# A hybrid recurrent and convolution layer on Trainium2: GpSimd's share of the first two thirds goes to VectorE and ScalarE, and the last head pair, its solve, the last conv block and the two recurrences are put in another order

## The chip, the cores and the metric

The kernel runs on one core of one Trainium2 chip. The metric is the device time of one execution in microseconds (us). Three runs of the kernel before took 1326.93, 1331.70 and 1330.41 us; the median is 1330.41. A separate execution was profiled, and every duration below comes from that one. The engines are named as the profile names them: PE is TensorE (matmuls) and PEld its weight loads, DVE is VectorE, ACT is ScalarE, POOL is GpSimd, SP is the engine that issues most DMAs. The granted clock is the fraction of TensorE's full clock that the chip allowed in a stretch of time.

## What is computed

One decoder layer over 1024 tokens of width 1024, all in float32: a norm, one input projection, then an eight-head recurrence on one part of the columns and a causal convolution of width 31 on the other, one output projection with a residual, and an MLP.

```python
def rwkv7_recurrence(r, decay, k, v, a_vec, b_vec):
    ...
    def step(S, inp):
        r_t, w_t, k_t, v_t, a_t, b_t = inp
        sa = jnp.einsum('bhvk,bhk->bhv', S, a_t)
        S = S * w_t[:, :, None, :] + sa[..., :, None] * b_t[:, :, None, :] + v_t[..., :, None] * k_t[:, :, None, :]
        y = jnp.einsum('bhvk,bhk->bhv', S, r_t)
        return S, y
...
def reference(x, ...):
    for l in range(DEPTH):
        h = rmsnorm(x, norm_mix_g[l])
        p = h @ w_in[l]
        p_rwkv = p[..., :D_RWKV_IN]
        p_rwkv = p_rwkv + (token_shift(p_rwkv) - p_rwkv) * shift_mu[l]
        p_conv = p[..., D_RWKV_IN:]
        y_rwkv = rwkv7_group(p_rwkv, ...)      # 8 heads of 64, with a group norm and a gate
        y_conv = conformer_conv_group(p_conv, ...)  # gated, 31 taps, layer norm, silu
        x = x + jnp.concatenate([y_rwkv, y_conv], axis=-1) @ w_out[l]
        h = rmsnorm(x, norm_mlp_g[l])
        x = x + jnp.square(jax.nn.relu(h @ w_ff1[l])) @ w_ff2[l]
    return rmsnorm(x, norm_final_g)
```

## The kernel before

**Projections.** A float32 product is made from three products of rounded halves: each operand is split into a high part (a rounded copy, made on ScalarE) and a low part (operand minus high part). `mm3` issues high x high, high x low and low x high for each of eight k-blocks, in matmuls of 128x128 weights by 256 columns. `load_w` (L214) loads 1024x128 input weights (`wraw`), makes `wh` on ScalarE (L219) and `wl` on GpSimd (L220); there are 22 such loads. `load_wout` (L682) does the same for the output weights in 16 pieces of 128x512 (`woh`, and `wol` on GpSimd, L692).

**Convolution.** Each of four conv blocks (`conv_block`, 128 channels) projects two weight blocks, gates them into `h`, and puts 31 taps into a list. `do_taps(n)` emits the next n of them: each is one VectorE instruction over 128x1024 (L317 the first, L319 the others) that adds onto `acc`. A tap that is emitted behind a solve is ordered behind the end of that solve (`gate`). When all taps are done, `conv_norm` (L639) normalises one half of the tokens: PE transposes, statistics on VectorE, scaling on ScalarE, PE transposes back, the activation (L663 to L665), and a split into high and low (`cvh` L668 on ScalarE, `cvl` L669 on GpSimd).

**Heads.** The eight heads are taken as four pairs, each in two halves of the tokens. `mix_block` projects and shifts r, k or v for a pair; `decays` (L390) makes the decay factors `E1` and `Ei`; `stage1` (L418) builds for each chunk of 64 tokens the small matrices that the recurrence needs: `AR` (L425, L426), `KB` (L437 and L439 on VectorE, and through `kq` on GpSimd, L436 and L440), their products `AM` (PE, masked on VectorE L448), the transposed, decayed `KB` called `kt` (a matmul of `KB` with a diagonal matrix `dg`, which GpSimd builds in L456), and a bonus term (L471 to L475, of which L472 on GpSimd). They go to DRAM (`lk_d`, `am_d`, `v_d`, `bon_d`).

**Solves.** The recurrence is computed in chunks, which takes the inverse of a triangular matrix for each. `solve(g)` does it for the two pairs of group g: a first product with `nup` (L501, shown as `Q<-Q,nup`), 60 small VectorE operations (L505 and L507), and a last product (L509). `merge(g, h)` puts the inverses' blocks together for one half of the tokens, through DRAM, with a VectorE transpose (`QT`, L524), 64 tiny matmuls and ScalarE copies.

**The two recurrences.** `step(g)` does one of 16 chunks of group g, each in three dependent hops in `chain` (L570): PE with `L1` then a ScalarE copy (L590), PE with `Th` then a copy (L596), PE with `KB` then a VectorE addition into the next chunk's `rhs` (L601). In the profile the matmuls of group 0 write `ca` and `ya`, those of group 1 `cb` and `yb`; their operands are called `rhs,LK`, `SR,TA` and `rhs,TA`. The state times the decay, `SR` (L585), is GpSimd's. `fetch` loads the chunk's matrices two chunks ahead into rings that both recurrences share (`LK` three buffers, `rhs` and `TA` two each). Recurrence 1 needs `solve(1)` and `merge(1)`, recurrence 0 `solve(0)` and `merge(0)`.

**Output projection and MLP.** `out_first` adds the convolution half onto x, `post` (L606) normalises and gates the recurrence's output (GpSimd adds the bonus, L629), and `out_second` adds that half. The MLP behind it is a blocked product whose operand sums run partly on GpSimd (L1187, L1310).

**What sets the order.** The function calls these pieces in a hand-written sequence near its end (L960 on). A scheduler then reorders instructions between engines by a simulated timeline and by priorities (`solve`, `merge` and `step` have a raised one), and the result is a fixed in-order queue for each engine. PSUM banks are handed out in turn from named cycles (L74).

## Time and profile before

| quantity | value |
|---|---|
| median of three runs | 1330.41 us |
| the profiled execution | 1334.43 us |
| its span, first to last instruction | 1332.7 us |
| PE busy | 1229.8 us (92%) |
| DVE busy | 960.9 us (72%) |
| ACT busy | 539.6 us (40%) |
| POOL busy | 291.1 us (22%) |
| mean granted clock | 0.961 |

The page divides the span into 40 slices of about 33 us. Each digit is the busy share in tenths; `PEclk` is the granted clock in tenths.

```profile
PE   6999899988998859999999999999948899999996
DVE  6379965698999672444669766665428898897997
ACT  6313233322323363333468454545533333433345
POOL 2124143332333153311000000000004324231420
PEclk9999899998998778999999999999978899999999
```

The recurrences and the output projection lie in slices 11 to 20, the MLP behind them. POOL is at work in the first 19 slices and again from slice 31 on.

### The profile page before, as it was taken

How to read it: one execution, taken by the hardware profiler on the slowest of the kernel's cores; microseconds unless marked ns; L12 is line 12 of the kernel's file. 1: busy time of each engine (PE TensorE's matmuls, PEld its weight loads, DVE VectorE, ACT ScalarE, POOL GpSimd, SP SyncE). 2: the span in 40 equal slices, each digit the busy share in tenths (PEclk: the TensorE clock that was granted, in tenths of full speed). 3: DMA queues.
4: the chain of work that ended last, by engine and by line, in shares of the span. 5: the costliest groups of instructions: out<-in, count | busy, mean ns of one | idle time of the engine just before them, and what ended most of it. 6: DMA issues, size and time to landing. Idle time of an engine off the chain costs nothing.

```text
span 1332.7 us, 20860 instructions
## 1 busy us (share of the span) xinstructions
PE 1229.8 (92%) x8171; PEld 1059.0 (79%) x8171; DVE 960.9 (72%) x1440; ACT 539.6 (40%) x937; POOL 291.1 (22%) x181
## 2 busy tenths in 40 slices
PE   6999899988998859999999999999948899999996
PEld 5999788887896748899988788888837688888885
DVE  6379965698999672444669766665428898897997
ACT  6313233322323363333468454545533333433345
POOL 2124143332333153311000000000004324231420
PEclk9999899998998778999999999999978899999999
DMA  5211445525626667536135554543157425223003
GB/s 185 56 48 37 109 112 145 132 72 122 155 59 158 160 162 186 176 112 178 44 110 183 159 162 142 163 134 124 66 167 267 142 80 158 63 81 93 16 1 126
DMA packets 194475, 161.44 MB, mean 121 GB/s; under 512 B 54387, under 2 KB 153785, under 8 KB 194377
## 3 DMA queue, kind: packets, MB, share of 16 engines
q1 hardware_dynamic: 181192, 157.90, 40.0%
q10 hardware_dynamic: 13056, 2.13, 0.9%
q8 instruction: 64, 1.05, 0.3%
q14 instruction: 35, 0.28, 0.1%
q0 software_dynamic: 128, 0.08, 0.0%
HBM read 110.23 MB, written 49.84 MB: 120 GB/s over the span
## 4 chain that ended last, share of the span: by engine, by line
PE 60%; DVE 24%; DMA 7%; issue 4%; ACT 2%; SPq 1%; POOL 1%; DVEq 0%; ACTq 0%
PE ps L96 27%; DVE acc L319 9%; PE yb L96 9%; PE ya L96 8%; PE cb L96 7%; PE ca L96 5%; PE pr L96 3%; DMA lk_d<-kt 2%; DVE Q L507 2%; DVE Qt L505 1%; DVE bl L827 1%; DVE sA L1187 1%; DVE al L827 1%; DVE ta L437 1%; PE ps L99 1%
## 5 line engine op out<-in xcount | busy, mean ns | idle before, releaser
L319 DVE SCALAR_TENSOR_TENSOR acc<-h,cw,acc 128x1024 f32<-128x1024 f32 x120 | 176.8, 1493 | 1.1
L826 ACT ACTIVATE ah<-sA 128x1024 fp32r<-128x1024 f32 x32 | 34.0, 1061 | 135.3 <-PE pr L96 50.1
L96 PE MATMUL ps<-bh,ah 128*128 128x512 f32 x168 | 65.7, 404 | 22.4 <-ACT bh L826 16.5
L220 POOL TENSOR_TENSOR wl<-wraw,wh 128x1024 fp32r<-128x1024 f32 x22 | 56.6, 2572 | 136.1 <-ACT wh L219 136.1
L1187 POOL TENSOR_TENSOR sB<-B,B11e 128x1024 f32<-128x1024 f32 x4 | 11.6, 2890 | 337.5 <-DMA B<-in_w_ff_dram 335.2
L96 PE MATMUL cb<-hh,wh 128*128 128x256 f32 x264 | 79.4, 301 | 5.1 <-DVE k L257 3.1
L96 PE MATMUL cb<-hl,wh 128*128 128x256 f32 x264 | 79.9, 302 | 0.1
L96 PE MATMUL cb<-hh,wl 128*128 128x256 f32 x264 | 77.8, 295 | 0.0
L96 PE MATMUL ps<-bl,ah 128*128 128x512 f32 x168 | 68.1, 405 | 4.0 <-DVE bl L827 3.9
L96 PE MATMUL yb<-hh,wl 128*128 128x256 f32 x248 | 71.5, 288 | 0.0
L96 PE MATMUL yb<-hh,wh 128*128 128x256 f32 x248 | 71.4, 288 | 0.0
L96 PE MATMUL yb<-hl,wh 128*128 128x256 f32 x248 | 71.0, 286 | 0.0
L96 PE MATMUL ps<-bh,al 128*128 128x512 f32 x168 | 67.5, 402 | 0.0
L827 DVE TENSOR_TENSOR al<-sA,ah 128x1024 fp32r<-128x1024 f32 x32 | 50.5, 1580 | 23.6 <-ACT ah L826 23.6
L827 DVE TENSOR_TENSOR w1l<-s,w1h 128x512 fp32r<-128x512 f32 x64 | 43.9, 687 | 24.8 <-ACT w1h L826 24.8
L826 ACT ACTIVATE w1h<-s 128x512 fp32r<-128x512 f32 x64 | 40.3, 632 | 50.5 <-PE ps L96 29.0
L96 PEld LDWEIGHTS cb<-hh,wh 128*128 128x128 f32 x264 | 53.2, 202 | 9.0 <-DVE k L257 3.3
L96 PEld LDWEIGHTS cb<-hl,wh 128*128 128x128 f32 x264 | 53.1, 201 | 4.8 <-issue 4.0
L96 PEld LDWEIGHTS ps<-bh,ah 128*128 128x128 f32 x168 | 32.9, 197 | 30.2 <-ACT bh L826 16.9
L585 POOL TENSOR_TENSOR SR<-rhs,PC 64x256 f32<-64x256 f32 x30 | 28.6, 953 | 124.8 <-DVE rhs L601 104.8
L96 PEld LDWEIGHTS cb<-hh,wl 128*128 128x128 f32 x264 | 53.3, 202 | 2.3 <-issue 2.0
L846 ACT ACTIVATE c<-c 128x512 f32<-128x512 f32 x60 | 38.0, 633 | 38.2 <-DVE c L932 21.5
(460 smaller groups left out, 4008.8 us busy)
## 6 DMA issues: line engine op xcount, KB each, us to landing
w1r<-in_w_ff_dram SPq DMA_DIRECT2D x44, 512.0 KB
hid_d<-c SPq DMA_DIRECT2D x64, 256.0 KB
LK<-lk_d SPq DMA_DIRECT2D x32, 384.0 KB
...
```

Of the source, the lines that this page charges most:

```text
L96: return self._order(PE.matmul(o, lhsT=lhsT, rhs=rhs, start=start, stop=stop, skip_group_check=more))
L99: self._order(PE.transpose(o, in_, identity))
L220: G.tensor_tensor(wl, raw, wh.bitcast(F32), op=ALU.subtract)
L319: return V.scalar_tensor_tensor(accs[cb], h2[:, j:j + T], cw[:, j, cb:cb + 1], accs[cb], op0=ALU.mult, op1=ALU.add)
L437: V.scalar_tensor_tensor(ta, ta, 1.0, Ei, op0=ALU.add, op1=ALU.mult)
L505: V.tensor_tensor(o, Q[:, 0:s, s:s + 1].to_broadcast([R, s, n]), Q[:, s:s + 1, s + 1:32].to_broadcast([R, s, n]), op=ALU.mult)
L507: V.tensor_tensor(Q[:, 0:s, s + 1:32], Q[:, 0:s, s + 1:32], o, op=ALU.add)
L585: G.tensor_tensor(SP, rhs[0:64], PC[:, c, 4 * g:4 * g + 4, None].to_broadcast([C, 4, C]), op=ALU.mult)
L826: S.activation(hi, src, AF.Copy)
L827: V.tensor_tensor(lo, src, hi.bitcast(F32), op=ALU.subtract)
L846: S.activation(c, c if src is None else src, AF.Relu)
L1187: engine.tensor_tensor(t, x, y, op=op)
```

## The change

There are three edits.

1. Every GpSimd arithmetic operation ahead of the MLP becomes a VectorE operation of the same shape: `wl` (22), `kq`, `KB` and `r` (8 each), `SR` (30), `yo` (8), `cvl` (8) and `wol` (16). GpSimd keeps its memsets, masks and DMA issues there, and its sums in the MLP.
2. `dg` goes. Four ScalarE operations per group of four chunks scale `KB` into `kd`, and PE transposes `kd`, where it multiplied `KB` by `dg`.
3. The hand-written order changes. The third conv block's projections move ahead of `solve(0)`. The fourth head pair's projections and stages move ahead of the fourth conv block. `solve(1)` and `merge(1)` come directly behind that block's projections, 23 of its taps behind `merge(1, 0)`'s call, and both convolution norms behind all of these. Recurrence 1 starts before the second convolution norm, its steps alternating with recurrence 0's. The cycles of PSUM banks are narrowed while both run.

```diff
-        G.tensor_tensor(wl, raw, wh.bitcast(F32), op=ALU.subtract)
+        V.tensor_tensor(wl, raw, wh.bitcast(F32), op=ALU.subtract)
...
-            dg = mp.tile([P, 4, P], F32, name="dg", bufs=1)
-            G.tensor_tensor(dg, ident[:, None, :].to_broadcast([P, 4, P]),
-                            E1[:, 4 * q:4 * q + 4, C:C + 1].to_broadcast([P, 4, P]), op=ALU.mult)
+            kd = mp.tile([P, 4, P], F32, name="kd", bufs=1)
+            for c in range(4):
+                S.activation(kd[:, c, :], KB[:, 4 * q + c].rearrange("p j t -> p (j t)"), AF.Copy, scale=E1[:, 4 * q + c, C:C + 1])
             bk = bank("s1")
             for c in range(4):
-                bk.mm(bk.t[:, c * P:(c + 1) * P], KB[:, 4 * q + c].rearrange("p j t -> p (j t)"), dg[:, c, :], True, True)
+                bk.tr(bk.t[:, c * P:(c + 1) * P], kd[:, c, :], ident)
...
-            G.tensor_tensor(SP, rhs[0:64], PC[:, c, 4 * g:4 * g + 4, None].to_broadcast([C, 4, C]), op=ALU.mult)
+            V.tensor_tensor(SP, rhs[0:64], PC[:, c, 4 * g:4 * g + 4, None].to_broadcast([C, 4, C]), op=ALU.mult)
...
     do_taps(2)
+    conv_block(2)
     solve(0, (0, 1))
     merge(0, 0)
     in_banks.append("inb")
-    do_taps(4)
-    do_taps(4)
-    conv_block(2)
+    do_taps(8)
     decays(2, 0)
...
-    conv_block(3)
...
     step(0)
     mix_block(7, (0, 1))
     mix_block(3, (0, 1))
+    step(0)
     mix_block(11, (0, 1))
+    do_taps(15)
+    step(0)
     stage1(3, 0)
     decays(3, 1)
+    step(0)
+    stage1(3, 1)
+    step(0)
+    conv_block(3)
     do_taps(8)
-    stage1(3, 1)
-    step(0)
-    step(0)
+    step(0)
+    solve(1, (0, 1))
+    step(0)
+    merge(1, 0)
+    step(0)
+    do_taps(23)
+    assert not taps
+    step(0)
+    merge(1, 1)
     step(0)
     done_in()
+    cycles["any"] = ("ps", "ps", "ps", "pr")
     ct = open_pool("ct", side="right")
     sc = open_pool("sc", side="right")
     cTs[0] = conv_norm(sc, ct, 0)
     close_pool("sc")
-    solve(1, (0, 1))
+    step(0)
     wo = open_pool("wo", side="right")
     load_wout(wo, wo, (4, 5, 6, 7))
-    merge(1, 0)
-    step(0)
-    merge(1, 1)
-    step(0)
-    step(0)
-    step(0)
+    step(0)
+    step(1)
+    step(0)
+    step(1)
     step(0)
     sc = open_pool("sc", side="right")
     cTs[1] = conv_norm(sc, ct, 1)
...
+    cycles["any"] = ("ps", "ca", "ps", "ya", "ps", "pr")
     out_first(wo, 0, 0)
-    step(1)
-    step(1)
     step(1)
```

**The end of the input projection.** The first two excerpts are TensorE's queue around the end of the input projection. `hh` and `hl` are the halves of the normed input, `wh` and `wl` those of the weights, so `cb<-hh_167,wh` is an input-projection matmul; `ps<-AR,KB` makes `AM`, `ps<-dg,KB` and `ps<-ident,kd` make `kt`, and `ca` and `ya` are recurrence 0. Before:

```order
L96 MATMUL cb<-hh_171,wl 128x256
L96 MATMUL ps<-sqk,sel_684 2x512
L96 MATMUL ca<-rhs,LK 64x64 x4
L96 MATMUL ya<-rhs,LK 64x64 x4
L96 MATMUL ps<-AR,KB 128x128 x11
L96 MATMUL ca<-SR,TA 64x64 x4
L96 MATMUL ps<-AR,KB 128x128 x5
L96 MATMUL ca<-rhs,LK 64x64 x4
L96 MATMUL ya<-rhs,TA 64x64 x4
L96 MATMUL ps<-dg,KB 128x128 x4
```

After, around the last `AR,KB` of the last pair's last half:

```order
L96 MATMUL cb<-hh_167,wh 128x256
L96 MATMUL cb<-hl_168,wh 128x256
L96 MATMUL cb<-hh_167,wl 128x256
L96 MATMUL ps<-AR,KB 128x128 x4
L96 MATMUL cb<-hh_171,wh 128x256
L96 MATMUL cb<-hl_172,wh 128x256
L96 MATMUL ca<-SR,TA 64x64 x4
L96 MATMUL cb<-hh_171,wl 128x256
L96 MATMUL cb<-hh_143,wh 128x256
L99 MATMUL ps<-ident,kd 128x128 x4
```

Before, the last input-projection matmul (the first row) stood ahead of both last stages of the fourth pair, and these had only recurrence steps between their matmuls. Now the fourth conv block's projection stands between them.

**Behind the second solve.** The next two excerpts are VectorE's queue from the last small operation of `solve(1)` on. Before:

```order
L507 TENSOR_TENSOR Q<-Q,Qt 128x30
L509 TENSOR_TENSOR Q<-Q,nup 128x1024
L665 SCALAR_TENSOR_TENSOR hn<-th_5107,hn 128x512
L665 SCALAR_TENSOR_TENSOR hn<-th_5121,hn 128x512
L524 STREAM_TRANSPOSE QT<-QS 128x256
L665 SCALAR_TENSOR_TENSOR hn<-th_5135,hn 128x512
L665 SCALAR_TENSOR_TENSOR hn<-th_5149,hn 128x512
L699 TENSOR_TENSOR x_0_4448<-xr,ps 128x512
L524 STREAM_TRANSPOSE QT<-QS 128x256
L699 TENSOR_TENSOR x_2_4450<-xr,ps 128x512
L601 TENSOR_TENSOR rhs<-cb,SR 64x256 x3
```

After:

```order
L507 TENSOR_TENSOR Q<-Q,Qt 128x30
L509 TENSOR_TENSOR Q<-Q,nup 128x1024
L319 SCALAR_TENSOR_TENSOR acc<-h_4120,cw,acc 128x1024
L601 TENSOR_TENSOR rhs<-ca,SR 64x256
L319 SCALAR_TENSOR_TENSOR acc<-h_4120,cw,acc 128x1024 x4
L524 STREAM_TRANSPOSE QT<-QS 128x256
L319 SCALAR_TENSOR_TENSOR acc<-h_4120,cw,acc 128x1024 x8
L524 STREAM_TRANSPOSE QT<-QS 128x256
L319 SCALAR_TENSOR_TENSOR acc<-h_4120,cw,acc 128x1024
L601 TENSOR_TENSOR rhs<-cb,SR 64x256
L319 SCALAR_TENSOR_TENSOR acc<-h_4120,cw,acc 128x1024
L585 TENSOR_TENSOR SR<-rhs,PC 64x256 x2
```

Before, the end of the second convolution norm (`hn`) and the first additions of the output projection (L699) stood directly behind the solve, since all taps were done. Now 23 taps stand there, with recurrence 1's first addition (`rhs<-cb`) among them; the convolution norms follow behind the taps. In the whole queue, 10 of recurrence 0's additions stood ahead of this solve's first product before, and 4 do now.

**The start of the output projection.** The last two excerpts are TensorE's queue there. `woh` and `wol` are the output weights' halves, `cvh` and `cvl` those of the normed convolution, so `ps<-woh_4690,cvh_4533` is an output-projection matmul; `QT,MX` and `QS,PT` belong to `merge(1, ...)`, and `cb` and `yb` are recurrence 1. Before:

```order
L99 MATMUL ps<-ident,yc_5043 128x128
L96 MATMUL cb<-QT,MX 32x32 x32
L96 MATMUL ps<-woh_4690,cvh_4533 128x256
L96 MATMUL cb<-QS,PT 32x32 x32
L96 MATMUL ps<-wol_4691,cvh_4533 128x256
L96 MATMUL ps<-woh_4690,cvl_4534 128x256
L96 MATMUL ps<-woh_4696,cvh_4547 128x256
L96 MATMUL cb<-rhs,LK 64x64 x4
```

After:

```order
L96 MATMUL cb<-SR,TA 64x64 x4
L99 MATMUL ps<-ident,yc_5165 128x128
L99 MATMUL ps<-ident,yc_5166 128x128
L99 MATMUL ps<-ident,yc_5167 128x128
L99 MATMUL ps<-ident,yc_5168 128x128
L96 MATMUL cb<-rhs,LK 64x64 x4
L96 MATMUL yb<-rhs,TA 64x64 x4
L96 MATMUL ps<-woh_4966,cvh_4855 128x256
```

Before, the first output-projection matmul stood ahead of recurrence 1's first hop. Now eight of that recurrence's additions stand ahead of it, among the transposes of the convolution norms (`ident,yc`).

More of the change, by code (lines that the diff above doesn't have):

```diff
@@ L435, in stage1 @@
         S.activation(kq, ta, AF.Identity, scale=kah[:, p:p + 1], bias=kac[:, p:p + 1])
-        G.tensor_tensor(kq, kq, k, op=ALU.mult)
+        V.tensor_tensor(kq, kq, k, op=ALU.mult)
         V.scalar_tensor_tensor(ta, ta, 1.0, Ei, op0=ALU.add, op1=ALU.mult)
@@ L439, in stage1 @@
         V.scalar_tensor_tensor(KB[:, :, 0, :], c8(k), kr, c8(ta), op0=ALU.mult, op1=ALU.mult)
-        G.tensor_tensor(KB[:, :, 1, :], c8(kq), c8(Ei), op=ALU.mult)
+        V.tensor_tensor(KB[:, :, 1, :], c8(kq), c8(Ei), op=ALU.mult)
         for i in range(2):
@@ L471, in stage1 @@
         S.activation(r, r, AF.Copy, scale=prm("r_k", p))
-        G.tensor_tensor(r, r, kq, op=ALU.mult)
+        V.tensor_tensor(r, r, kq, op=ALU.mult)
         bb = bank("s1")
@@ L628, in post @@
             S.activation(yo[:, p, :], b.t[:, p * P:(p + 1) * P], AF.Identity, scale=prm("ln_x_g", p), bias=prm("ln_x_b", p))
-        G.tensor_tensor(yo, yo, bon, op=ALU.add)
+        V.tensor_tensor(yo, yo, bon, op=ALU.add)
         V.tensor_tensor(yo, yo, bg.t.rearrange("p (n t) -> p n t", n=NP), op=ALU.mult)
@@ L668, in conv_norm @@
             S.activation(ch, hn, AF.Copy)
-            G.tensor_tensor(cl, hn, ch.bitcast(F32), op=ALU.subtract)
+            V.tensor_tensor(cl, hn, ch.bitcast(F32), op=ALU.subtract)
             res.append((ch, cl))
@@ L691, in load_wout @@
                 S.activation(wh, raw, AF.Copy)
-                G.tensor_tensor(wl, raw, wh.bitcast(F32), op=ALU.subtract)
+                V.tensor_tensor(wl, raw, wh.bitcast(F32), op=ALU.subtract)
                 wos[k, n] = wh, wl
@@ L1002, in hymba_layer @@
     stage1(2, 1)
-    do_taps(4)
-    do_taps(4)
-    do_taps(4)
-    do_taps(4)
+    do_taps(16)
     decays(3, 0)
-    do_taps(4)
-    do_taps(4)
-    step(0)
-    do_taps(4)
-    do_taps(3)
-    step(0)
-    step(0)
-    step(0)
-    step(0)
-    conv_block(3)
-    do_taps(4)
-    do_taps(4)
-    do_taps(4)
-    do_taps(4)
-    do_taps(4)
-    do_taps(4)
-    do_taps(3)
     step(0)
@@ L1027, in hymba_layer @@
     mix_block(3, (0, 1))
+    step(0)
     mix_block(11, (0, 1))
+    do_taps(15)
+    step(0)
     stage1(3, 0)
     decays(3, 1)
-    do_taps(8)
+    step(0)
     stage1(3, 1)
     step(0)
+    conv_block(3)
+    do_taps(8)
     step(0)
+    solve(1, (0, 1))
[6 more added lines that the diff above has]
+    merge(1, 1)
     step(0)
     done_in()
+    cycles["any"] = ("ps", "ps", "ps", "pr")
     ct = open_pool("ct", side="right")
@@ L1040, in hymba_layer @@
     close_pool("sc")
-    solve(1, (0, 1))
+    step(0)
     wo = open_pool("wo", side="right")
     load_wout(wo, wo, (4, 5, 6, 7))
-    merge(1, 0)
     step(0)
-    merge(1, 1)
+    step(1)
     step(0)
-    step(0)
-    step(0)
+    step(1)
     step(0)
@@ L1062, in hymba_layer @@
     step(0)
+    assert steps[0] == 16
+    cycles["any"] = ("ps", "ca", "ps", "ya", "ps", "pr")
     out_first(wo, 0, 0)
-    step(1)
-    step(1)
     step(1)
@@ L1077, in hymba_layer @@
     post(op, 1)
-    do_taps(4)
-    do_taps(4)
     out_first(wo, 3, 1)
@@ L1095, in hymba_layer @@
     out_first(wo, 4, 1)
-    do_taps(4)
     step(1)
@@ L1130, in hymba_layer @@
     close_pool("nx")
+    assert steps[1] == 16
     ph2.close()
+    cycles["any"] = ("ps", "ca", "ya", "ps", "cb", "pr", "ps", "yb")
     fpb = open_pool("fpb", side="right")
```

## The prediction

> **What bounds the kernel now.** I read the page's head and its chain of work first, then the busy time of each engine by stage, then who TensorE waited for.
>
> ```profile
> span 1332.7 us, 20860 instructions
> PE 60%; DVE 24%; DMA 7%; issue 4%; ACT 2%; SPq 1%; POOL 1%; DVEq 0%; ACTq 0%
> 0.00:451.45 451.45, 410.59 (x3349) 368.48 (x3350) 351.44 (x457) 141.61 (x273) 136.66 (x97) 0.95 0.41 107
> 451.45:505.03 53.58, 35.72 (x447) 28.37 (x446) 41.50 (x117) 35.07 (x65) 22.97 (x21) 0.80 0.62 165
> 505.03:690.00 184.97, 181.22 (x1756) 168.03 (x1756) 87.33 (x243) 70.43 (x169) 33.18 (x33) 0.99 0.49 139
> 690.00:1332.70 642.70, 602.29 (x2625) 494.10 (x2623) 480.62 (x624) 292.53 (x432) 98.33 (x32) 0.97 0.38 122
> 403.00:451.45 48.45, 41.56 (x326) 32.65 (x325) 37.46 (x40) 13.99 (x30) 13.79 (x13) 0.79 0.60 149
> ```
>
> A row gives the stretch, its length, the busy time of PE, PEld, DVE, ACT and POOL, the granted clock and the DMA share. I cut where the work changes: 403 is the end of the last input-projection matmul, 451.45 the start of the second solve, 505.03 the point from which output-projection matmuls run without gaps, 690 about where the MLP begins. The chain that ended last runs 60% over TensorE and 24% over VectorE, so these two are cut up by stage. TensorE is the bound almost everywhere: 410.6 of 451.5 us, then 181.2 of 185.0. It is not in the second row, 35.7 of 53.6 us at a clock of 0.80, nor in the last row, the end of the first stage: 41.6 of 48.5 at 0.79. The time to be won before the MLP is the time in which TensorE idles or runs at a reduced clock. The MLP keeps its order and its engines, so I cost it at nothing.
>
> ```profile
> PE pr L99 <- DVE xt L233: 10.6, 3, 9.7
> PE ps L96 <- DVE KB L439: 7.0, 4, 2.6
> PE ps L96 <- ACT kt L462: 5.1, 3, 3.6
> PE cb L96 <- DVE QT L524: 4.8, 1, 4.8
> PE ps L96 <- DVE AM L448: 3.6, 2, 2.1
> ```
>
> This is TensorE's waiting up to 660 us (total, times, longest). No row names POOL: GpSimd was never what TensorE waited for last in these rows. What GpSimd costs is seen on VectorE.
>
> ```profile
> L319 DVE SCALAR_TENSOR_TENSOR acc<-h,cw,acc 128x1024 f32<-128x1024 f32 x120 | 176.8, 1493 | 1.1
> L319 DVE SCALAR_TENSOR_TENSOR acc<-h,cw,acc x120: 1239/1276/3533, 75.2 to 435.3; 128x1024 f32<-128x1024 f32 x120
> L437 DVE SCALAR_TENSOR_TENSOR ta<-ta,Ei 128x512 f32<-128x512 f32 x8 | 14.5, 1810 | 0.0
> L437 DVE SCALAR_TENSOR_TENSOR ta<-ta,Ei x8: 675/1222/5904, 113.1 to 429.9; 128x512 f32<-128x512 f32 x8
> ```
>
> The same tap takes 1.24 to 3.5 us, the same L437 0.68 to 5.9 us. Over the typical tap the 120 taps lose 120 x (1493 - 1276) = 26 us; over its shortest, L437 loses 8 x (1810 - 675) = 9 us. So 35 us of VectorE's 480 before 690 is stretching by something beside it, and two-input operations running while GpSimd runs fit that. The Trainium skill, "SBUF — State Buffer", section "Who interferes with whom", says that a VectorE operation with two SBUF inputs and a GpSimd operation that reads SBUF block each other for whole instructions; by that rule up to POOL's 136.7 us before 451 would come back to VectorE, an estimate; the two rows above show 35 of it, and the sum goes by those.
>
> **Edit 1: GpSimd's work goes to VectorE.**
>
> ```profile
> L220 POOL TENSOR_TENSOR wl<-wraw,wh x22: 2354/2438/3456, 10.4 to 379.2; 128x1024 fp32r<-128x1024 f32 x22
> L436 POOL TENSOR_TENSOR kq<-kq,k 128x512 f32<-128x512 f32 x8 | 14.2, 1779 | 35.2 <-ACT kq L435 22.6 <-DVE k L257 12.6
> L585 POOL TENSOR_TENSOR SR<-rhs,PC x30: 606/607/2787, 201.9 to 642.9; 64x256 f32<-64x256 f32 x30
> L692 POOL TENSOR_TENSOR wol<-woraw,woh 128x512 fp32r<-128x512 f32 x16 | 20.7, 1298 | 29.1 <-ACT woh L691 16.8 <-DMA woraw<-in_w_out_dram 4.6 <-DMA xr<-in_x_dram 4.2
> L827 DVE TENSOR_TENSOR al<-A,ah x16: 1208/1217/1226, 1001.4 to 1295.5; 128x1024 fp32r<-128x1024 f32 x16
> L827 DVE TENSOR_TENSOR w1l<-w1r,w1h x48: 673/686/695, 619.9 to 973.5; 128x512 fp32r<-128x512 f32 x48
> L601 DVE TENSOR_TENSOR rhs<-ca,SR x7: 407/417/417, 440.1 to 480.9; 64x256 f32<-64x256 f32 x7
> L601 DVE TENSOR_TENSOR rhs<-cb,SR x10: 406/417/418, 514.3 to 599.7; 64x256 f32<-64x256 f32 x10
> ```
>
> The lower four rows are VectorE doing the same shapes. So VectorE takes on 22 x 1.22 = 26.8 us (wl), 24 x 0.69 = 16.5 us (kq, KB and r), 30 x 0.42 = 12.5 us (SR) and 32 x 0.69 = 22 us (yo, cvl, wol): 78 us, less the 35 us of stretching, net +43 over 690 us (480 to 523, 76%). In the first stage it is 26.8 + 16.5 + some 2 for SR, less nearly all of the 35: about +10 on 351 of 451 us. The cover is TensorE's own 411 us; it holds while no wl sits long behind taps. KB becomes ready earlier, since its two products on the way (kq, KB) take 0.69 instead of some 1.8 us. At the start a wl stands inside the first normalisation's chain (wl starts at 10.4 today, the first scaling at 8.8):
>
> ```profile
> L233 DVE TENSOR_SCALAR xt<-xt,rs x8: 740/746/2222, 8.8 to 30.7; 128x1024 f32<-128x1024 f32 x8
> ```
>
> Waiting for that wl ends at 10.4 + 1.2 = 11.6, some 3 us behind 8.8; the second tile's scaling is late today too, so between 0 and +3.4 us; I take **+1**.
>
> **Edit 2: kd for dg.** The matmuls stay as many and as large (128x128).
>
> ```profile
> L456 POOL TENSOR_TENSOR dg<-ident,E 128x512 f32<-128x512 f32 x16 | 20.5, 1282 | 88.5 <-PE ps L96 50.5 <-ACT E L411 38.0
> L628 ACT ACTIVATE yo<-ca,par x32: 448/458/466, 537.9 to 674.2; 128x128 f32<-128x128 f32 x32
> ```
>
> ScalarE takes 64 more, at most 0.46 us each by L628 (which reads PSUM): 29 us on 142 busy of 451. They stand between KB and the transposes, which dg did not; each stage has two groups of four, 1.8 us a group, hidden where input projection fills TensorE. Only in the fourth pair's last half is little of it left: between 0 and 2 x 1.8 = 3.6 us; I take **0**.
>
> **Edit 3: the order.** In front, the fourth head pair now comes ahead of the last conv block, so that block's matmuls stand between its stages. Today nothing but stages and recurrence steps stand behind 403, and the last row of the first fence prices the hole: 6.9 us idle and 0.21 x 48.5 = 10 us of clock, overlapping in part: 7 to 17 us, I take 14. In the rest of the front, KB's and AM's waits (7.0 + 3.6) and 12 us of reduced clock (0.05 x 451 = 22.6, less those 10) are to be had in part: 0 to 22, I take 9. Together **-23** (7 to 39).
>
> Behind the front, these rows mark today's serial stage:
>
> ```profile
> 451.45 1.53 DVE L501 TENSOR_TENSOR Q<-Q,nup 128x1024 f32<-128x1024 f32 x1 [0.24 <-DMA Q<-am_d]
> 489.97 1.23 DVE L509 TENSOR_TENSOR Q<-Q,nup 128x1024 f32<-128x1024 f32 x1
> 505.03 0.41 PE L96 MATMUL ps<-woh,cvh 128*128 128x256 f32 x1
> 514.28 0.42 DVE L601 TENSOR_TENSOR rhs<-cb,SR 64x256 f32<-64x256 f32 x1
> L507 DVE TENSOR_TENSOR Q<-Q,Qt 128x30 f32<-128x30 f32 (+14 forms) x30 | 12.1, 404 | 0.3
> L505 DVE TENSOR_TENSOR Qt<-Q 128x30 f32<-128x30 f32 (+14 forms) x30 | 11.0, 366 | 0.4
> 455.69 0.68 PE L96 MATMUL ca<-rhs,LK 128*64 128x64 f32 x8 [0.67 <-ACT rhs L596]
> 456.30 0.67 PE L96 MATMUL ya<-rhs,TA 64*64 64x64 f32 x8
> 458.08 0.67 PE L96 MATMUL ca<-SR,TA 64*64 64x64 f32 x8 [0.17 <-ACT SR L590]
> 459.26 0.68 PE L96 MATMUL ca<-rhs,LK 128*64 128x64 f32 x8 [0.51 <-ACT rhs L596]
> ```
>
> Today: solve from 451.5 to 491.2, convolution norm beside it, output projection dense at +53.6; all taps are done at 436. Changed, 32 taps are left when the second solve starts, 9 inside it and 23 held behind it, and the convolution norm comes behind the last tap. On VectorE: the solve's 60 small operations 23.1 us (the L507 and L505 rows), two Q products 2.5, 9 taps at 1.28 = 11.5, eight steps' rhs and SR 16 x 0.42 = 6.7: **44**. Then 23 taps, 29.4, with two QT, four rhs and five SR, 4.7, and a wait of some 2 for the first rhs of the second recurrence (514.3 - 491.2 = 23 us behind the solve today): **36**. Then convolution norm, for which I take the ACT time of today's stage, 35.1, which holds the same two norms and some recurrence copies: **34**. Sum 114, or **+60** on 53.6.
>
> What that buys: the matmuls of one step fill about 2.9 us of the 3.6 from 455.69 to 459.26. Before the second solve only 4 additions of the first recurrence are done instead of 10: 6 x 2.9 = **-17** in a stage where TensorE was the bound. Behind the start of output projection 8 steps of the second recurrence are already done: 8 x 2.9 = **-23** in a stage that was 98% busy; and of its 3.8 us idle I take **-3**. The output weights' loads stand on SP's queue behind fetches that wait for ring buffers; they have the serial stage's length as cover.
>
> Sum: +60 - 17 - 23 - 23 - 3 + 1 = **-5 us**: 1334.4 of the profiled execution (span 1332.7) becomes about 1329. The shown median, 1330.4, lies 4 below that execution, so I write **1325**.
>
> **Rivals.** *Slower: the steps set the serial stage.* VectorE's queue is in order, and eight rhs stand in the solve, eight more before the first output matmul. Today's L601 rows give 6.8 us a step without filler (40.8 us for 6 intervals) and 9.5 beside output projection (85.4 for 9). Decisive are 44/8 = 5.5 us in the solve and (70 - 23)/7 = 6.7 behind it. At 6.8 and 8.2 the stage is 54 + 23 + 57 = 134 instead of 114: +20, **1345** (at 9.5 it is 54 + 23 + 66, or +29: **1354**). For it speaks the clock:
>
> ```profile
> 460.00:480.00 20.00, 15.35 (x168) 12.04 (x167) 19.38 (x46) 15.21 (x28) 10.26 (x9) 1.00 0.40 108
> 480.00:500.00 20.00, 9.13 (x113) 6.93 (x113) 12.68 (x41) 12.19 (x21) 8.73 (x7) 0.60 0.80 213
> 431.32 1.11 PE L96 MATMUL ca<-SR,TA 64*64 64x64 f32 x8
> ```
>
> Where TensorE was half idle the clock was 0.60, and a hop took 1.11 instead of 0.67, so a step's three hops gain 1.3 us. Against it, steps at 15.4 of 20 busy kept 1.00, and ACT and VectorE's norm work is no longer beside the solve. The Trainium skill, "TensorE: Matmul & The Clock Gate", section "HAM oscillation — how this bites in real kernels", says that a gap of about 3.4 us puts the clock at half until work is sustained; taken for all 16 steps of the stage that is 16 x 1.3 = 21 us, or 1346, an estimate, and the row from 460 to 480 shows that steps alone need not fall under it.
>
> *Faster: VectorE's relief reaches TensorE.* If the front gives 39 instead of 23, and the serial stage's taps run at their 1.24 minimum (32 x 0.04 = 1) with no wait for the first rhs (2), the result is 19 lower: **1306**. For it: the stretched L437 stands directly ahead of KB, TensorE's largest wait after the start. Against: TensorE is at 95% clock and 91% busy there already.
>
> *Nothing or a little slower: VectorE's queue takes what GpSimd gave.* A wl behind one tap comes up to 1.28 us later, 22 times, 28 us at most; it decides once wl is later than TensorE's weight order needs. If the front then gives 8 instead of 23, the result is 15 higher: **1340**.
>
> **How the numbers follow.** About 0.5%, 6.7 us, is what a measurement can tell from no change. Forecast 0.44 (1314 to 1336), of which 0.26 is faster by more than that and 0.18 within it; the faster rival 0.18; steps 0.22, of which 0.02 within 0.5%; VectorE's queue 0.16, of which 0.06. So faster 0.44, same 0.26 (0.18 + 0.02 + 0.06), slower 0.30. The range takes in the slow rival at 9.5 us a step with 3 us of kd's bound (1357), and the faster one with a norm part a third shorter, since ScalarE's 35 us hold copies and weights that are not the norm's, and with the start at 0 instead of +1 (1306 - 11 - 1 = 1294, set at 1290): 1290 to 1357.
>
> **What would show it.** Hardly a POOL row ahead of the MLP; the tap's mean near 1.28; L437 near 0.7; the clock near 1.00 from the end of the front's waits to the second solve, and that start near 412 (451.5 - 17 - 23 + 1). Then 32 taps behind it, the first dense output matmul some 114 us later (526), and 159 us instead of 185 from there to the MLP. The step rival shows as VectorE idle for `ca` or `cb` inside the solve, with rhs rows over 6 us apart; the queue rival as TensorE waiting for wl. Wrong altogether would be a start of the solve behind 430, or an MLP of other length than 643 us.

## The result, and the profile after

The changed kernel takes 1312.62 us in the median of four runs (1312.27 to 1315.79), the kernel before 1331.03 beside it. The ratio is 0.9873, with a 95% interval from 0.9848 to 0.9899: 1.3% faster. The forecast was 1325, 0.4% faster, with 1290 to 1357 as its range. The profiled execution's span is 1310.6 us, 22.1 less than before. One run of those below is left out as slow, 1420.88 us at a granted clock of 0.82 in `e5_no_kd`, whose median is that of the other nine.

First the head of the page after, its chain of work and two rows of the slices (POOL and the clock, then a digit for each fortieth of the span).

```profile
span 1310.6 us, 20752 instructions
PE 82%; DVE 6%; DMA 6%; ACT 3%; issue 1%; SPq 1%; ACTq 0%; DVEq 0%
POOL 1000000000000000000000000000004324232320
PEclk9999999999996588999999999999978899999998
```

VectorE's share of the chain that ended last fell from 24% to 6%, and TensorE's rose from 60% to 82%: ahead of the second solve, TensorE waits for only some 7 us in all behind its first wait. The clock row has lost its dips in slices 5 and 10. Slices 13 to 16, 8 7 7 8 before, are 6 5 8 8 now: the new serial stage lies there.

Next the busy time by stage after: the stretch, its length, PE, PEld, DVE, ACT and POOL busy, the granted clock and the DMA share. I cut at the second solve's start (385.5) and end (427.5), the end of the last tap (461.7), the output projection and about where the MLP begins.

```profile
0.00:385.50 385.50, 364.20 (x3058) 330.11 (x3059) 285.69 (x470) 155.24 (x323) 5.79 (x24) 1.00 0.45 117
385.50:427.50 42.00, 34.92 (x341) 29.84 (x339) 37.62 (x91) 8.42 (x23) 0.30 (x1) 0.72 0.56 151
427.50:461.70 34.20, 23.78 (x411) 21.36 (x412) 32.39 (x34) 4.12 (x12) 0.00 (x0) 0.56 0.54 117
461.70:510.00 48.30, 39.01 (x388) 32.79 (x388) 27.50 (x74) 35.41 (x67) 0.00 (x0) 0.85 0.61 176
510.00:670.00 160.00, 157.18 (x1312) 147.07 (x1312) 94.40 (x260) 65.62 (x154) 0.00 (x0) 0.99 0.41 122
```

The marks come from these rows of the timeline after: the solve's first and last product, the last tap, the first output-projection matmul and the last addition of the output projection.

```profile
385.50 1.23 DVE L501 TENSOR_TENSOR Q<-Q,nup 128x1024 f32<-128x1024 f32 x1 [0.66 <-DMA Q<-am_d]
426.32 1.23 DVE L509 TENSOR_TENSOR Q<-Q,nup 128x1024 f32<-128x1024 f32 x1
460.37 1.27 DVE L319 SCALAR_TENSOR_TENSOR acc<-h,cw,acc 128x1024 f32<-128x1024 f32 x1
504.80 0.58 PE L96 MATMUL ps<-woh,cvh 128*128 128x256 f32 x1
667.66 0.69 DVE L699 TENSOR_TENSOR x<-x,ps 128x512 f32<-128x512 f32 x1 [1.95 <-PE ps L96]
```

I use four numbers for each kernel from here on: the start of the second solve; the time from there to the *dense* output projection (the first of thirteen matmuls by the high weights `woh` that start within 6 us); from there to the end of the last addition; and the rest of the span. For the kernel before, the last two marks are these rows:

```profile
504.81 0.42 PE L96 MATMUL ps<-woh,cvl 128*128 128x256 f32 x1
687.83 0.69 DVE L699 TENSOR_TENSOR x<-x,ps 128x512 f32<-128x512 f32 x1 [1.72 <-PE ps L96]
```

| | second solve starts | to dense output projection | to the last addition | rest |
|---|---|---|---|---|
| before | 451.4 | 53.4 | 183.7 | 644.2 |
| after | 385.5 | 119.3 | 163.5 | 642.3 |
| difference | -65.9 | +65.9 | -20.2 | -1.9 |
| forecast | -39 | +60 | -26 | 0 |

The sum is -22.1 us of the profiled span, where -5 was forecast. The front gave 27 us more than expected, the serial stage cost 6 more, and the output projection gave 6 less.

VectorE's rows after show the relief. First come groups of instructions with their busy time and mean.

```profile
L319 DVE SCALAR_TENSOR_TENSOR acc<-h,cw,acc 128x1024 f32<-128x1024 f32 x120 | 152.1, 1279 | 1.0
L425 DVE SCALAR_TENSOR_TENSOR AR<-k,nkk,E 128x512 f32<-128x512 f32 x8 | 5.9, 741 | 0.5 <-issue 0.5
L507 DVE TENSOR_TENSOR Q<-Q,Qt 128x30 f32<-128x30 f32 (+14 forms) x60 | 19.7, 328 | 1.4
L505 DVE TENSOR_TENSOR Qt<-Q 128x30 f32<-128x30 f32 (+14 forms) x60 | 19.6, 327 | 2.9 <-issue 1.6
```

Then two lines by themselves, with their shortest, median and longest.

```profile
L319 DVE SCALAR_TENSOR_TENSOR acc<-h,cw,acc x120: 1242/1282/1297, 77.6 to 460.4; 128x1024 f32<-128x1024 f32 x120
L437 DVE SCALAR_TENSOR_TENSOR ta<-ta,Ei x8: 676/686/693, 109.7 to 363.1; 128x512 f32<-128x512 f32 x8
```

Before, over the same part of the program, three of the groups, and that of L426, read:

```profile
L425 DVE SCALAR_TENSOR_TENSOR AR<-k,nkk,E 128x512 f32<-128x512 f32 x8 | 14.3, 1787 | 2.0 <-ACT E L411 1.6 <-issue 0.3
L507 DVE TENSOR_TENSOR Q<-Q,Qt 128x30 f32<-128x30 f32 (+14 forms) x60 | 24.9, 414 | 1.2
L505 DVE TENSOR_TENSOR Qt<-Q 128x30 f32<-128x30 f32 (+14 forms) x60 | 24.0, 400 | 1.2
L426 DVE TENSOR_TENSOR AR<-r,E 128x512 f32<-128x512 f32 x8 | 9.6, 1200 | 0.3 <-issue 0.3
```

No tap is longer than 1.30 us any more, no L437 longer than 0.69. L425 alone lost 8 us that way before, and the solves' small operations 10; neither was in my estimate.

TensorE's longest waits up to 660 us after (total, times, longest):

```profile
PE pr L99 <- DVE xt L233: 13.9, 1, 13.9
PE cb L96 <- DMA TA<-th_d: 5.8, 2, 5.1
PE cb L96 <- DVE QT L524: 3.6, 1, 3.6
PE ca L96 <- ACT rhs L596: 3.2, 7, 0.5
```

KB and AM, 10.6 us before, are gone from the list. All rows but the first belong to the serial stage.

### The profile page after: what moved, and what is told of

Its sections match the earlier page's. It is cut to its first block, busy times and chain, and to the rows that moved or that the text cites. A ratio compares the mean times of both kernels' runs of the same rounds, so it can differ in the third digit from the quotient of the medians.

```text
span 1310.6 us, 20752 instructions
## 1 busy us (share of the span) xinstructions
PE 1218.1 (93%) x8107; PEld 1053.5 (80%) x8107; DVE 956.1 (73%) x1548; ACT 558.9 (43%) x1001; POOL 100.7 (8%) x57
## 4 chain that ended last, share of the span: by engine, by line
PE 82%; DVE 6%; DMA 6%; ACT 3%; issue 1%; SPq 1%; ACTq 0%; DVEq 0%
PE ps L96 30%; PE yb L96 14%; PE cb L96 12%; PE ya L96 11%; PE ca L96 9%; PE pr L96 3%; PE ps L99 1%; DVE al L827 1%; DVE sA L1177 1%; DVE acc L319 1%; DMA lk_d<-kt 1%; DMA xt<-in_x_dram 1%; DMA rhs<-v_d 1%; DVE x L1208 1%; DMA th_d<-QS 1%
## 5 line engine op out<-in xcount | busy, mean ns | idle before, releaser
L319 DVE SCALAR_TENSOR_TENSOR acc<-h,cw,acc 128x1024 f32<-128x1024 f32 x120 | 152.1, 1279 | 1.0
L96 PE MATMUL ps<-bh,ah 128*128 128x512 f32 x168 | 65.9, 405 | 21.4 <-ACT bh L826 16.6
L96 PE MATMUL cb<-hh,wh 128*128 128x256 f32 x248 | 72.7, 293 | 1.5 <-ACT hh L243 1.5
L827 DVE TENSOR_TENSOR al<-sA,ah 128x1024 fp32r<-128x1024 f32 x32 | 55.5, 1734 | 23.5 <-ACT ah L826 23.5
L96 PE MATMUL cb<-hl,wh 128*128 128x256 f32 x248 | 71.9, 290 | 0.2 <-DVE hl L244 0.2
L96 PE MATMUL cb<-hh,wl 128*128 128x256 f32 x248 | 71.8, 289 | 0.0
L96 PEld LDWEIGHTS cb<-hh,wh 128*128 128x128 f32 x248 | 48.0, 193 | 6.3 <-issue 2.7
L96 PEld LDWEIGHTS cb<-hl,wh 128*128 128x128 f32 x248 | 47.8, 193 | 3.5 <-issue 2.8
L96 PEld LDWEIGHTS cb<-hh,wl 128*128 128x128 f32 x248 | 47.9, 193 | 2.1 <-issue 1.8
L219 ACT ACTIVATE wh<-wraw 128x1024 fp32r<-128x1024 f32 x22 | 23.2, 1056 | 60.5 <-PE cb L96 31.8
L96 PEld LDWEIGHTS yb<-hh,wh 128*128 128x128 f32 x232 | 44.5, 192 | 5.1 <-issue 4.1
```

Source lines behind the costliest of these rows:

```text
L96: return self._order(PE.matmul(o, lhsT=lhsT, rhs=rhs, start=start, stop=stop, skip_group_check=more))
L219: S.activation(wh, raw, AF.Copy)
L319: return V.scalar_tensor_tensor(accs[cb], h2[:, j:j + T], cw[:, j, cb:cb + 1], accs[cb], op0=ALU.mult, op1=ALU.add)
L827: V.tensor_tensor(lo, src, hi.bitcast(F32), op=ALU.subtract)
```

## The experiments

The kernels below are variants of one of the two. Ratios are to the kernel before, timed on the same chip, with 95% intervals. The scheduler plans the whole order anew for each kernel, so an edit also moves instructions that it doesn't touch; the additions of recurrence 0 that stand ahead of the second solve (10 before, 4 after) are told where they differ, since each step is about 2.9 us of TensorE work.

### Each edit alone

`e1_engines`: the kernel before, with all eight kinds of operations on VectorE.

```diff
-        G.tensor_tensor(wl, raw, wh.bitcast(F32), op=ALU.subtract)
+        V.tensor_tensor(wl, raw, wh.bitcast(F32), op=ALU.subtract)
...
-            G.tensor_tensor(SP, rhs[0:64], PC[:, c, 4 * g:4 * g + 4, None].to_broadcast([C, 4, C]), op=ALU.mult)
+            V.tensor_tensor(SP, rhs[0:64], PC[:, c, 4 * g:4 * g + 4, None].to_broadcast([C, 4, C]), op=ALU.mult)
```

> The kernel before with edit 1 alone (GpSimd's eight kinds of operations on VectorE; dg stays on GpSimd, order as before). Theory A, contention: the front lost its time because GpSimd beside VectorE stretched taps, L437, L426 and KB and so starved TensorE; then taps come near 1.28 us, the granted clock ahead of the second solve goes from 0.95 towards 1.00, the second solve starts 25 to 40 us earlier than 451 (410 to 427), and the total is 20 to 35 us lower (1295 to 1310). Theory B, order: the front's gain came from the fourth conv block as filler; then the taps get shorter but the second solve starts within 8 us of 451 and the total stays within 8 us of before.

Measured: 1330.91 us, ratio 0.9996 (0.9975 to 1.0018). The front went A's way, but less far than A asked: the second solve starts at 429.7, 22 us earlier instead of 25 to 40 (8 additions ahead of it instead of 10), the taps' mean falls from 1.49 to 1.30 us, and the granted clock up to the solve stays at 0.95. The total did what B says. Behind the solve's start, 64.0 us to the dense output projection and 195.7 to the last addition stand where 53.4 and 183.7 stood: all 22 us are given back.

`e2_kd`: the kernel before with kd for dg (edit 2 of the diff).

> The kernel before with edit 2 alone (kd on ScalarE and PE transposes in place of dg on GpSimd and matmuls). The profile after shows 64 PE records of kd where dg had 128. Theory A (cheaper PE work counts, TensorE being the bound in front): 5 to 8 us less TensorE work ahead of the second solve and up to 8 us off the total (1322 to 1328). Theory B (it is hidden): total within 4 us of before.

Measured: 1325.31 us, ratio 0.9947 (0.993 to 0.9964), second solve at 439.7 with the same 10 additions ahead. A holds: TensorE is busy for 405.6 us ahead of the second solve, 5 less than the 410.6 before. Its ground is seen in these rows. First the group of kd's transposes in the changed kernel:

```profile
L99 PE MATMUL ps<-ident,kd 128*128 128x128 f32 x64 | 13.6, 279 | 0.0
```

Then the group of dg's matmuls in the kernel before, and behind it one bank's four matmuls in its timeline:

```profile
L96 PE MATMUL ps<-dg,KB 128*128 128x128 f32 x128 | 19.9, 302 | 0.9 <-POOL dg L456 0.9
```

```profile
447.17 1.16 PE L96 MATMUL ps<-dg,KB 128*128 128x128 f32 x8
```

The trace has two records for each float32 matmul by dg, and one for each float32 transpose. I had written that the matmuls stay as many and as large.

`e3_order`: the changed kernel with edits 1 and 2 undone, so the new order alone.

> The changed kernel with edits 1 and 2 undone: the new order alone, with GpSimd's operations and dg as before. Theory A (contention): the new order alone wins only the 6 steps moved and the hole behind 403 in front (second solve at 415 to 425), pays the longer serial stage of 114 to 125 us, and ends 5 to 25 us slower than before (1336 to 1356). Theory B (order): the front is as short as in the changed kernel (second solve at 385 to 395) and the total is within 8 us of 1313.

Measured: 1366.31 us, ratio 1.0241 (1.0201 to 1.028), second solve at 438.8 with 7 additions ahead, 132.4 us from there to the dense output projection. A's sign is right and its size too small: the new order by itself costs 34 us, and the second solve starts later than A's 415 to 425. Its taps and its front show where. First all its taps, then its first 300 us and the rest of the front by engine.

```profile
L319 DVE SCALAR_TENSOR_TENSOR acc<-h,cw,acc x120: 1235/1274/3829, 75.0 to 517.2; 128x1024 f32<-128x1024 f32 x120
```

```profile
0.00:300.00 300.00, 272.18 (x1989) 250.53 (x1990) 216.79 (x326) 100.17 (x186) 89.24 (x65) 0.95 0.36 99
300.00:438.80 138.80, 129.04 (x1183) 111.02 (x1182) 97.12 (x96) 38.27 (x78) 40.85 (x29) 0.89 0.52 125
```

With GpSimd at work beside them the taps still stretch to 3.8 us, and although the filler now stands between the last stages, the clock from 300 us to the second solve is 0.89, where it was 0.91 before and is 1.00 in the changed kernel.

`e4_engines_kd`: edits 1 and 2 under the old order.

> The kernel before with edits 1 and 2, order as before. If the edits add up (A), this gives 25 to 43 us less than before (1288 to 1306) and beats the changed kernel, since the serial stage stays at about 54 us while the front runs at full clock. If the order is what won (B), it stays within 10 us of before.

Measured: 1339.96 us, ratio 1.0051 (1.0029 to 1.0074). The edits do not add up: both together are slower than either alone. B's total holds, at 8 us over before, but not by B's front: that is again short (427.3), and 69.4 and 200.8 us follow. Neither theory gave this size for the loss behind the solve.

### kd or no kd under the new order

`e5_no_kd`: the changed kernel with dg on GpSimd again.

> The changed kernel with edit 2 undone (dg on GpSimd and its 128 matmul records; all else as changed). Theory A (kd earns its place under the new order, since TensorE has 64 records fewer and VectorE is never stretched): 5 to 12 us slower than the changed kernel, 1318 to 1325, the second solve at 391 to 397. Theory B (dg's 16 operations of 1.05 us are too few to matter): within 4 us of 1313.

Measured: 1337.30 us, ratio 1.0038 (1.0017 to 1.0059): 25 us slower than the changed kernel by the medians, 22 by the ratios, beyond A's bound. The second solve starts at 407.3, later than A's 397, with 6 additions ahead, and 130.5 us follow instead of 119.3. The profiled execution took 1342.79 us, the longest of the nine.

`e10_dg_act`: dg stays, but ScalarE builds it, so that no GpSimd arithmetic is left beside the taps.

```diff
-            kd = mp.tile([P, 4, P], F32, name="kd", bufs=1)
+            dg = mp.tile([P, 4, P], F32, name="dg", bufs=1)
             for c in range(4):
-                S.activation(kd[:, c, :], KB[:, 4 * q + c].rearrange("p j t -> p (j t)"), AF.Copy, scale=E1[:, 4 * q + c, C:C + 1])
+                S.activation(dg[:, c, :], ident, AF.Copy, scale=E1[:, 4 * q + c, C:C + 1])
...
-                bk.tr(bk.t[:, c * P:(c + 1) * P], kd[:, c, :], ident)
+                bk.mm(bk.t[:, c * P:(c + 1) * P], KB[:, 4 * q + c].rearrange("p j t -> p (j t)"), dg[:, c, :], True, True)
```

> The changed kernel with dg back, but built by four ScalarE operations from the identity, not on GpSimd: no GpSimd operation beside the taps, but 128 matmul records instead of 64. Theory A (kd's gain is TensorE's shorter work): second solve at 393 to 408, total 8 to 26 us over the changed kernel (1321 to 1339). Theory B (it was dg's place on GpSimd): second solve within 4 us of 385.5, total within 4 us of 1313.

Measured: 1332.82 us, ratio 0.9998 (0.9974 to 1.0022), second solve at 400.7. A's numbers hold: GpSimd is out and 20 us of the 25 are still lost. This is its front:

```profile
0.00:300.00 300.00, 284.59 (x2202) 262.61 (x2203) 212.32 (x376) 120.83 (x246) 5.56 (x22) 0.99 0.40 109
300.00:400.70 100.70, 94.81 (x1016) 81.21 (x1003) 76.01 (x99) 35.27 (x83) 0.22 (x2) 0.98 0.58 140
```

The clock is as good as after, TensorE as busy; it only has more to do. Eight dg records take 1.16 us in the row at 447.17 above (`e2_kd`), the last one some 0.28 of it, so they start 0.13 us apart, and 64 more are some 8 us; 6 additions ahead of the solve instead of 4 are 5.8: together 14 of the 15.2 us by which the solve starts later. The other part of the loss is the 130.1 us behind, 11 more than after, under another plan of the order. So the run shows that dg's place on GpSimd is not what most of the loss hangs on; that it is TensorE's longer work, as A says, is worked out for 8 us of it, and the rest comes with the planned order.

### What sets the serial stage

`e6_fewer_taps`: the changed kernel with 7 taps instead of 23 behind the second solve. It leaves out the other 16, so it does not compute the whole layer and only times the stage.

```diff
-    do_taps(23)
+    del taps[:16]
+    do_taps(7)
     assert not taps
```

> The changed kernel without 16 of the 23 taps that stand behind the second solve (the convolution's last block lacks 16 of its 31 taps). Theory A (VectorE's queue sets the serial stage): the stage from the second solve to the dense output projection shrinks from 119 by 14 to 20.5 us (16 x 1.28) and the total with it, 1292 to 1299. Theory B (the steps of the recurrences set it): the stage shrinks by less than 8 us.

Measured: 1306.96 us, ratio 0.9818 (0.979 to 0.9846), some 6 us less than the changed kernel. The last tap ends 22.2 us earlier, at 439.4, close to A's 16 x 1.28 = 20.5; the dense output projection starts only 10 us earlier, at 494.6, between A's 14 and B's 8. Between these two lie 55.2 us instead of 43.2:

```profile
439.40:494.60 55.20, 43.06 (x527) 37.79 (x527) 27.18 (x74) 35.32 (x67) 0.00 (x0) 0.65 0.56 146
484.39 0.42 DVE L601 TENSOR_TENSOR rhs<-cb,SR 64x256 f32<-64x256 f32 x1 [0.20 <-PE cb L96]
```

So VectorE's queue sets the stage up to the last tap, and something else behind it. The last row is recurrence 1's fourth addition, and its fifth comes at 500.7: only four of its steps stand ahead of the output projection here, where eight do in the changed kernel, and yet the stretch behind the last tap is longer. Four more steps are left for the output projection, which takes 5.7 us more (169.2).

`e9_norm_dve`: the norm's two scalings on VectorE instead of ScalarE.

```diff
-            S.activation(yc[t], yc[t], AF.Identity, scale=crs[:, t:t + 1], bias=nmr[:, t:t + 1])
+            V.tensor_scalar(yc[t], yc[t], crs[:, t:t + 1], nmr[:, t:t + 1], op0=ALU.mult, op1=ALU.add)
...
-            S.activation(hn, b.t, AF.Identity, scale=clgh[:, cb:cb + 1], bias=clbh[:, cb:cb + 1])
+            V.tensor_scalar(hn, b.t, clgh[:, cb:cb + 1], clbh[:, cb:cb + 1], op0=ALU.mult, op1=ALU.add)
```

> The changed kernel with the norm's two scalings (L655 and L663, 16 ScalarE operations of 0.78 us) on VectorE, which is idle for 21 of the 48 us behind the last tap. Theory A (behind the last tap the recurrences' copies stand in ScalarE's queue among the norm's operations, and that sets the stage): the steps there come closer than today's 8.1 us, the stage from last tap to dense output projection shrinks from 43 by 5 to 12 us, total 1301 to 1308. Theory B (TensorE's half clock and the hops' own length set it): stage within 3 us, total within 3 us of 1313.

Measured: 1317.74 us, ratio 0.9891 (0.9838 to 0.9944), not to be told from the changed kernel. The changed kernel from its last tap to the first output matmul, and then this one:

```profile
461.60:504.80 43.20, 33.91 (x360) 28.03 (x359) 23.98 (x69) 31.29 (x60) 0.00 (x0) 0.90 0.59 170
```

```profile
460.10:501.10 41.00, 30.93 (x340) 25.86 (x337) 30.39 (x80) 20.46 (x43) 0.00 (x0) 0.91 0.61 175
```

ScalarE lost 11 us of work there and the stretch 2, and the dense output projection started 7 us later than in the changed kernel (511.5). Recurrence 1's first eight additions still lie 8.2 us apart. ScalarE's queue alone doesn't set it: theory A falls.

`e7_out_early`: the first output weights are loaded ahead of the first norm, and two output blocks are emitted ahead of the second.

```diff
     ct = open_pool("ct", side="right")
+    wo = open_pool("wo", side="right")
+    load_wout(wo, wo, (4, 5, 6, 7))
     sc = open_pool("sc", side="right")
     cTs[0] = conv_norm(sc, ct, 0)
...
+    out_first(wo, 2, 1)
+    out_first(wo, 0, 0)
     sc = open_pool("sc", side="right")
     cTs[1] = conv_norm(sc, ct, 1)
```

> The changed kernel with the first output weights loaded ahead of the first convolution norm and two output-projection blocks emitted ahead of the second norm. In the changed kernel 43 us lie between the last tap and the first output matmul (461.6 to 504.8), of which the second norm is the later half. Theory A (the second norm, ahead in TensorE's and ScalarE's queues, held the output projection back): first output matmul 12 to 18 us earlier, TensorE idles less there, total 5 to 14 us lower, 1299 to 1308. Theory B (recurrence 1's eight steps hold it): output matmuls start earlier but the total stays within 4 us of 1313.

Measured: 1327.27 us, ratio 0.997 (0.9953 to 0.9986). The output projection starts 7 us earlier after the solve (112.4) and takes 20 us more (183.9). The solve's row and the output projection's show both sides of it.

```profile
385.20:438.10 52.90, 41.47 (x378) 35.84 (x377) 43.00 (x100) 13.40 (x31) 0.30 (x1) 0.63 0.62 172
497.60:681.50 183.90, 173.99 (x1483) 161.09 (x1482) 106.83 (x291) 80.98 (x180) 0.00 (x0) 0.96 0.41 119
```

The solve lasts 52.9 us where it lasted 42.0, with the output weights' work now among its operations. This is its row in that stretch:

```profile
L692 DVE TENSOR_TENSOR wol<-woraw,woh 128x512 fp32r<-128x512 f32 x8 | 5.5, 686 | 5.2 <-ACT woh L691 4.6 <-DMA xr<-in_x_dram 0.4
```

Its 5.5 us of work and the 5.2 us that VectorE waits ahead of it are the 10.9 us by which the solve is longer, all but 0.2. The earlier output projection has 10 us of idle TensorE. Neither theory foresaw a loss.

`e8_pe_taps`: as `e7_out_early`, with 8 of the last block's taps as matmuls by diagonal matrices.

```diff
+        for i, j in enumerate(js):
+            S.activation(dt_[:, i, :], ident, AF.Copy, scale=cw[:, j, cb:cb + 1])
...
+                b.mm(b.t, dt_[:, i, :], h2[:, j + 512 * h:j + 512 * h + 512], i == 0, i == n - 1)
...
+            V.tensor_tensor(accs[cb][:, s], accs[cb][:, s], bs[h].t, op=ALU.add)
```

> As e7_out_early, and 8 of the last block's taps done as matmuls with diagonal matrices (ScalarE scales the identity by the tap's weight) while TensorE idles in the serial stage, added to acc with two VectorE additions. Theory A (VectorE's queue sets the stage): 8 x 1.28 - 2 x 0.69 = 8.9 us less on VectorE, the clock there rises, and the total is 6 to 11 us under e7_out_early. Theory B (steps set it): within 3 us of e7_out_early.

Measured: 1324.73 us, ratio 0.9929 (0.9905 to 0.9953). The stage is 106.0 us, 6.4 less than in `e7_out_early`, and the output projection 3.9 longer. The ratios' intervals just touch. By the medians it gained 2.5 us, which is B's; by the ratios 5.5, just under A's 6 to 11. The totals don't decide between the two.

### Which of the eight operations

`e11_front_engines`: the kernel before with only wl, kq, KB and r on VectorE; SR, yo, cvl and wol stay on GpSimd, and so does dg.

> The kernel before with only wl, kq, KB and r on VectorE; SR, yo, cvl and wol stay on GpSimd, order as before. With all eight moved the second solve started 22 us earlier and the total did not move. Theory A (the later operations in VectorE's queue gave it back: cvl, wol and SR between the solve's and the norm's operations): total 10 to 20 us under before, 1311 to 1321. Theory B (the old order gives it back, whatever the engine, because recurrence 1 and the output projection keep their length): total within 5 us of before.

Measured: 1315.96 us, ratio 0.9871 (0.9841 to 0.9901): **as much as the whole change gains, from four kinds of operations moved**, under the old order. First `e1_engines` up to the second solve and from there to the dense output projection, then this kernel.

```profile
0.00:429.70 429.70, 402.51 (x3295) 363.47 (x3296) 333.11 (x507) 141.50 (x270) 26.06 (x40) 0.95 0.43 112
429.70:493.70 64.00, 40.81 (x495) 32.04 (x495) 49.71 (x145) 37.35 (x69) 0.30 (x1) 0.78 0.56 153
```

```profile
0.00:429.40 429.40, 398.97 (x3298) 361.35 (x3299) 332.87 (x500) 140.96 (x269) 45.34 (x50) 0.95 0.43 112
429.40:485.50 56.10, 39.77 (x486) 32.42 (x485) 42.90 (x118) 33.55 (x62) 17.73 (x18) 0.80 0.58 161
```

The fronts are alike. With the later four on VectorE, that engine has 49.7 us of work in the solve's stage instead of 42.9, and the stage is 8 us longer; the output projection is 7.6 longer too (195.7 against 188.1). So A: under the old order these four give the front's gain back.

`e12_late_gpsimd`: the same in the new order, that is the changed kernel with SR, yo, cvl and wol back on GpSimd.

> The changed kernel with SR, yo, cvl and wol back on GpSimd (wl, kq, KB and r stay on VectorE, kd and the new order stay). Under the old order this difference was worth 15 us (1330.9 to 1316.0). Theory A (these four kinds hold VectorE's queue in the solve and the norm, in either order): 5 to 15 us under the changed kernel, 1298 to 1308, by a stage from the second solve to the dense output projection shorter than 119. Theory B (in the new order that stage is set by steps and ScalarE, and GpSimd beside the last 32 taps stretches them again): between 4 us under and 10 us over the changed kernel, 1309 to 1323, with taps behind the second solve over 1.3 us in the mean.

Measured: 1320.58 us, ratio 0.9905 (0.9885 to 0.9926). No gain here, if anything a small loss: B in the total, and in its taps too, though these explain little of it. The taps behind the second solve's start, first by shortest, median and longest, then with their mean:

```profile
L319 DVE SCALAR_TENSOR_TENSOR acc<-h,cw,acc x30: 1264/1284/1522, 385.3 to 463.1; 128x1024 f32<-128x1024 f32 x30
L319 DVE SCALAR_TENSOR_TENSOR acc<-h,cw,acc 128x1024 f32<-128x1024 f32 x30 | 39.7, 1325 | 0.6
```

Their mean is 1.33 us, over the 1.3 that B asked for, and none is over 1.52; in the changed kernel the mean over the same stretch is 1.28, so 30 taps lose some 1.5 us. The last one ends 3 us later than in the changed kernel, and the dense output projection starts 11 us later; what makes up the rest isn't shown.

## Why the prediction was right, and where it was off

The sign was right and the time lay in the range. The sum was right only in part, and its terms were off in both directions: the front gave 27 us more than its term, the stages behind it 12 less, and that they partly cancel is luck. What happened is closer to the faster rival, VectorE's relief reaching TensorE (39 us in front, 1306), than to the forecast, with part of the slower rival's loss on top. KB and AM are gone from TensorE's waits, and in front it is busy for 364 of 385.5 us at a clock of 1.00.

**The relief of VectorE was mis-sized, and that is the largest error.** "So 35 us of VectorE's 480 before 690 is stretching" counted the two rows that I had picked. VectorE took on 78 us of work, as forecast, and yet its busy time up to the output projection's end did not rise: 285.7 + 37.6 + 32.4 + 27.5 + 94.4 = 478 us after, against 480 before. So some 80 us of stretching went, not 35: 25 from the taps and 9 from L437 as counted, and the rest from rows left out, such as L425 (14.3 to 5.9), L505 and L507 (48.9 to 39.3) and L426 (9.6 to 5.5). The rule of the Trainium skill, "SBUF — State Buffer", section "Who interferes with whom", that the two engines share a pair of SBUF ports under an exclusive lock, gave up to 137 us in the prediction, for GpSimd's work ahead of 451 us. Up to 690 us, where the 80 are counted, GpSimd was busy for 136.7 + 23.0 + 33.2 = 193 us, so the 80 measured lie between that bound and my rows, and agree with the rule's direction.

**The front's term, -23, should have been -49**, the solve's 65.9 us less the 17 of the moved steps (its bounds were 7 to 39). The start's +1 held: the 192nd input-projection matmul starts at 51.0 us instead of 49.8. Following one path through the runs, each by one profiled execution that lies up to 5.5 us above its kernel's median, the new order alone moves the second solve from 451.4 to 438.8, the eight operations from there to 407.3, and kd from there to 385.5. I had given the order 14 for its filler, the relief 9 and kd nothing. The 12.6 of the order are mostly its three fewer steps (8.7), so the filler alone brought some 4 of its 14; that it pays only once VectorE can feed the stages fits the clock of 0.89 in `e3_order`, but no run shows it by itself. The engines are worth 31.5 with one step moved in them (2.9), and kd 21.8 with two (5.8).

**"The matmuls stay as many and as large" was wrong.** 128 records became 64. `e10_dg_act` shows that dg's place on GpSimd is the smaller part of kd's worth: 20 of 25 us stay lost without it. The 64 records account for some 8 of these 20, and the rest comes with another planned order.

**The serial stage, 114, is 119.** Its first two parts are close: solve 42.0 (44), taps 34.1 (36), both with VectorE busy 38 of 42 and 32 of 34 us at a clock of 0.72 and 0.56, so the low clock that spoke for the slower rival decided nothing there: the solve's eight steps come 5.0 us apart, under the rival's 5.5. The third, the norm, took 43.2 instead of 34. There the steps are as slow as the rival said, as recurrence 1's first and eighth addition after show:

```profile
447.51 0.42 DVE L601 TENSOR_TENSOR rhs<-cb,SR 64x256 f32<-64x256 f32 x1
504.09 0.41 DVE L601 TENSOR_TENSOR rhs<-cb,SR 64x256 f32<-64x256 f32 x1
```

From 447.5 to 504.1 its steps lie 8.1 us apart, over the 6.7 that I had named as decisive, and these seven intervals, 56.6 us, are the rival's 57. That the steps are what holds the output projection back isn't shown, though: in `e6_fewer_taps` only four of them stand ahead of it, and the stretch behind the last tap grew from 43.2 to 55.2 us. Nor is it settled what makes a step take 8 us: it isn't ScalarE's load alone (`e9_norm_dve`), and the fetches' ring and the reduced clock (0.90 behind the last tap, 0.65 in `e6_fewer_taps`) weren't tried by themselves.

**The output projection gave 20, not 26.** Its stretch is TensorE's, 157.2 of 160 us, as said. From its dense start to its last addition TensorE's work fell by 19.3 us (179.9 to 160.7), where eight steps had been put at 23, and its idle time by 1 (3.8 to 2.8), where I had taken 3.

**VectorE's queue taking what GpSimd gave** was the third rival. Its mechanism, TensorE waiting for wl, did not come. Under the old order a neighbour of it did: the later operations in VectorE's queue cost 15 us (`e1_engines` against `e11_front_engines`). Under the new one they did not.

**What stays open.** The three edits do not add up, in either order: edits 1 and 2 together cost 8 us under the old order and save 54 under the new. The runs show where the time lies, stage by stage, but part of each difference behind the second solve (130 against 119 us with and without kd) comes with another planned order, and no run held the order fixed. The old order with the four front operations and kd, or with a later split of SR, yo, cvl and wol, wasn't tried; no kernel here that computes the whole layer beats the changed one.
